# Moving the split weights of 256-column and 512-column products to different byte offsets in SBUF

## The chip, the cores and the metric

The kernel runs on one core of a Trainium2 chip. The metric is the device time of one execution in microseconds (us). Engines are called as in the profile: PE is TensorE (the matmuls; PEld is its loading of stationary weights), DVE is VectorE, ACT is ScalarE, POOL is GpSimd, SP is SyncE, which here only issues DMAs. SBUF is the on-chip memory of 128 partitions; an offset below is a number of bytes within one partition.

## The reference

One layer of a decoder trunk on x of 512 tokens by 1024, all in float32. Cut to what matters:

```python
h = rms_norm(x, g_mix)
qa, ka, va, qb, kb, vb, gates = split(h @ w_in)
ya = moba_attention(rope(qa), rope(ka), va)        # 8 heads of 64
yb = stick_breaking_attention(qb, kb, vb)          # 8 heads of 64
g = sigmoid(gates + b_gate)
x = x + (g[0] * (ya @ w_branch_a) + g[1] * (yb @ w_branch_b)) @ w_out
u = causal_depthwise_conv(rms_norm(x, g_ffn) @ w_up, conv_w, conv_b)
x = x + (silu(u_gate) * u_val) @ w_down            # w_up: 1024 x 5632, w_down: 2816 x 1024
return rms_norm(x, g_final)
```

Nearly all the work is in the products with w_in, w_branch, w_out, w_up and w_down.

## The kernel before

**Products.** Every float32 operand of a large product is split into two float32r tiles, `hi` (ACT copies the raw tile, line 74, 661 or 981) and `lo` = raw - hi (DVE, line 75, 661 or 983). `mm3` (lines 78 to 81) then makes three matmuls of each product: hi with hi, hi with lo, lo with hi. Each matmul has its own stationary operand of 128 by 128 (a block of 512 bytes in each partition), loaded while the matmul before streams its moving operand of 256 or 512 columns (1024 or 2048 bytes in each partition). The order of the matmuls on PE is the order of the program.

**Weights.** A DMA from SP brings a raw weight tile of 128 by 1024 into one of five `raw` buffers. The split weights `whi` and `wlo`, 4096 bytes each, come from the pool `wsp` (line 61), three buffers of each name in rotation. In some stages a split goes to other pools (`osp`, `dsp`) instead. The users of `wsp` are

- `wload` (line 62), for the first projections, the value projections, the queries, keys and gates, the branch products and the plain columns of w_up;
- `split_in` (line 658), for w_out and w_down;
- `upload` (line 803), for the first four tiles of w_up;
- `wmix` (line 972), for the mixed columns of w_up. For the last of its four tiles, `wd` (line 1004), hi and lo share one `whi` buffer.

**Which products have 256 columns.** Three places:

- `vproj_b` (line 301), the values of the second attention: the weights are the moving operand, the activations `xg` the stationary one. 2 groups x 4 token tiles x 8 blocks x 3 = 192 matmuls, spread as fillers between the steps of the attention.
- `up_half` (line 854), the first four tiles of w_up: the weights are stationary, half of `h2` moves. 4 tiles x 2 halves x 8 blocks x 3 = 192 matmuls; one of the four tiles lies in `osp`, the other three in `wsp`, so 144 of them read `wsp`.
- `first_four` and `last_three` (lines 986 and 1001), the mixed stage, 16 columns of tiles (`MIXED`, 4 to 19) that are computed with seven quarter products in place of eight: the weights are stationary, and quarters of `h2` or sums of them in `tm4` (called xa in the profile) move. 16 x 7 quarters x 4 blocks x 3 = 1344 matmuls, one after the other.

That makes 1728 matmuls of 256 columns, 1680 of them with weights from `wsp`. The other large products move 512 columns: 1461 matmuls with weights from `wsp` (weights stationary in `proj`, `up_mm` and the branch products, moving in the first value projection and in the products with w_out and w_down), and some 490 with weights from `osp` and `dsp` or none.

**Addresses.** In the program as laid out, all six buffers of `wsp`, and also `xg`, `h2`, `tm4`, `osp`, `dsp` and the split activations, begin at 320 bytes modulo 512. So every weight block and every activation block that meet in a product have the same offset modulo 512.

**What orders the work around.** SP loads raw tiles ahead, up to five; ACT copies as soon as a `whi` buffer comes free, which is when PE has done the last matmul on it; DVE subtracts after ACT; PE takes the tiles in program order. During the mixed stage, POOL issues loads and stores of its own. Of the mixed tiles, `wc` gets its `lo` by DMA from DRAM (`wlo<-ulo`), where an earlier stage has put it.

Of the kernel before, what the change touches and what calls it, by code (L numbers as in the profile page):

```python
# [10 lines left out]
F32 = mybir.dt.float32  # L11
F32R = mybir.dt.float32r
# [15 lines left out]
NP = FT // 2  # L28
# [11 lines left out]
          + [("di", j, i) for j in DSUM for i in range(3)])  # L40
WIDX = {k: i for i, k in enumerate(WORDER)}
NEG = -1e30


@with_exitstack
def trunk_layer(ctx: ExitStack, tc: tile.TileContext, x: bass.AP, xT: bass.AP, w: bass.AP, vec: bass.AP,
# [3 lines left out]
    def pool(stack, name, bufs, space=None, side=None):  # L50
        kw = {}
        if space is not None:
            kw["space"] = space
        if side is not None:
            kw["side"] = side
        return stack.enter_context(tc.tile_pool(name=name, bufs=bufs, reuse_waits="tile", **kw))
# [1 line left out]
    ctx.enter_context(tc.manual_schedule(engines={mybir.EngineType.PE}))  # L58
    consts = pool(ctx, "consts", 1)
    wraw = pool(ctx, "wraw", 5)  # L60
    wsp = pool(ctx, "wsp", 3)
    def wload(key, pieces=1, eng=None):
        raw = wraw.tile([128, 1024], F32, name="raw")
        hi = wsp.tile([128, 1024], F32R, name="whi")
        lo = wsp.tile([128, 1024], F32R, name="wlo")
        n = 1024 // pieces
        for i in range(pieces):
            sl = slice(i * n, (i + 1) * n)
            (eng if eng is not None and i == 0 else nc.sync).dma_start(raw[:, sl], w[WIDX[key]][:, sl])
            if eng is not None and i == 0:  # L70
                nc.scalar.preload_act_table_set("sqrt_and_others")
        for i in range(pieces):
            sl = slice(i * n, (i + 1) * n)
            wload.hi = nc.scalar.activation(hi[:, sl], raw[:, sl], AF.Copy)  # L74
            wload.lo = nc.vector.tensor_sub(lo[:, sl], raw[:, sl], hi[:, sl].bitcast(F32))  # L75
        return hi, lo

    def mm3(ps, a, b, start, stop, **kw):
        nc.tensor.matmul(ps, a[0], b[0], start=start, stop=False, **kw)  # L79
        nc.tensor.matmul(ps, a[0], b[1], start=False, stop=False, **kw)  # L80
        nc.tensor.matmul(ps, a[1], b[0], start=False, stop=stop, **kw)  # L81

    def blk(t, k, n=128):
        return t[0][:, k * n:(k + 1) * n], t[1][:, k * n:(k + 1) * n]
# [27 lines left out]
    vb = vp.tile([128, QT, 512], F32, name="vb")  # L112
# [34 lines left out]
    for n in NWARM:  # L147
        nc.tensor.matmul(warm[:, :n], warmb[:, :128], warmb[:, :n], start=True, stop=True)  # L148
    mf = xp.tile([128, 128], F32, name="mf", bufs=1)
    nc.gpsimd.memset(mf, 0.0)  # L150
    nc.gpsimd.affine_select(out=mf, in_=mf, pattern=[[-1, 128]], compare_op=OP.is_ge, fill=NEG, base=0,
                            channel_multiplier=1)
# [146 lines left out]
        yield 1.0  # L299

    def vproj_b(g):
        wt = tuple(wload(("vb", g, h)) for h in range(2))
        for t in range(QT):
            if t % 2 == 0:
                ps = pmm.tile([128, S], F32, name="mm")
            o = ps[:, (t % 2) * 256:(t % 2 + 1) * 256]
            for k in range(KT):
                a = (xg[k][:, 0, t * 128:(t + 1) * 128], xg[k][:, 1, t * 128:(t + 1) * 128])
                mm3(o, a, blk(wt[k // 4], k % 4, 256), k == 0, k == KT - 1)
                if k < KT - 1:  # L310
                    yield 0.5
            if t % 2:
                dst = vb[:, t - 1:t + 1, g * 256:(g + 1) * 256]
                nc.scalar.activation(dst[:, 0], ps[:, :256], AF.Copy, scale=r1[:, t - 1:t])
                nc.vector.tensor_scalar(dst[:, 1], o, r1[:, t:t + 1], None, op0=OP.mult)
            yield 0.5
# [216 lines left out]

    pend = {}
    fillers = [moba_qk(1), sb_qk(0), sb_qk(1), vproj_b(0), sb_qk(2), sb_qk(3), vproj_b(1)]
    fillers += [gates(i) for i in range(NG)]
    GAPS_A = (12, 0, 5, 5, 0, 5, 7, 5, 5)
# [61 lines left out]
    for i in range(KT):  # L599
# [5 lines left out]
        g = pend[i]  # L605
# [27 lines left out]
    t2 = [ocb.tile([128, 512], F32, name=f"ot{j}") for j in range(HP)]  # L633
# [6 lines left out]
    def rload(key):  # L640
        raw = wraw.tile([128, 1024], F32, name="raw")
        nc.sync.dma_start(raw, w[WIDX[key]])
        return raw
# [12 lines left out]
            next(todo, None)  # L656

    def split_in(p, raw):
        lo = p.tile([128, 1024], F32R, name="wlo")
        hi = p.tile([128, 1024], F32R, name="whi")  # L660
        splits.append((nc.scalar.activation(hi, raw, AF.Copy), nc.vector.tensor_sub(lo, raw, hi.bitcast(F32))))  # L661
        return hi, lo

# [5 lines left out]
    def first_pass(cq, j, n, xa, keys, t2, pools, last):  # L669
        if t2 is None:  # L670
            r1, r2 = (wraw.tile([128, 1024], F32, name="raw") for _ in range(2))
            nc.sync.dma_start(r2.rearrange("p (h c) -> p h c", h=2), keys[0][0:2].rearrange("h p c -> p h c"))
            nc.sync.dma_start(r1[:, :512], w[WIDX[keys[1]]][:, :512])
            nc.sync.dma_start(r1[:, 512:], keys[0][2])
        else:
            r0 = rload(keys[0])
            r1 = rload(keys[1])
            r2 = wraw.tile([128, 1024], F32, name="raw")
            nc.vector.tensor_add(r2, r0, r1)  # L679
            nc.vector.tensor_add(r1[:, 512:], r1[:, :512], r2[:, 512:])  # L680
            nc.scalar.activation(t2, r1[:, 512:], AF.Copy)
        w2 = split_in(pools[0], r2)
        w1 = split_in(pools[1], r1)
        for wt in (w2, w1):
            step(dsums if cq is oq else homes, wt[1][:, :1].bitcast(F32))
        steps = [("c22", 1, w2, 0), ("c21", 3, w2, 1), ("c11", 0, w1, 0), ("c12", 2, w1, 1)]
        if j == n - 1 and last:
            steps = steps[2:] + steps[1::-1]
        for m, b, wt, h in steps:
            prod(cq[m], xa, b, wt, h, j == 0, j == n - 1)  # L690
        return splits[-1]
# [109 lines left out]
    wup = []  # L801

    def upload(p):
        raw = rload(("up",) + upq.pop(0))
        wup.append((p.tile([128, 1024], F32R, name="whi"), p.tile([128, 1024], F32R, name="wlo"), raw))

    def upload_half(n, h):
        sl = slice(h * 512, (h + 1) * 512)
# [2 lines left out]
    def upload_hi(p):  # L811
        upload(p)
        nc.scalar.activation(wup[-1][0], wup[-1][2], AF.Copy)
# [5 lines left out]
    for j in range(HP):  # L819
# [7 lines left out]
        for n in ("c11", "c21") if j < HP - 1 else ("c21", "c11"):  # L827
# [3 lines left out]
    inline(*(lambda t=t: nc.vector.tensor_add(oq["c22"][t], oq["c22"][t], oq["u3", t]) for t in range(2)),  # L831
           *(lambda t=t: x1_add(t, 1) for t in (2, 3)), lambda: upload_hi(wsp))
    upload(wsp)
    inline(lambda: nc.scalar.activation(sqj[:, :1], padt[:, :1], AF.Sqrt), *(lambda t=t: x1_sq(t, 1) for t in (2, 3)))
    inline(*(lambda t=t, f=f: f(t, 0) for t in (2, 3) for f in (x1_add, x1_sq)), lambda: upload_lo(0))
# [44 lines left out]
    t2 = [gp.tile([128, 512], F32, name=f"t2{j}") for j in range(2)]  # L880
# [90 lines left out]

    def wmix(i, parts, n=1024, lo=None):
        raw = wraw.tile([128, 1024], F32, name="raw")
        hi = wsp.tile([128, 1024], F32R, name="whi")
        wlo = wsp.tile([128, 1024], F32R, name="wlo") if n == 1024 else hi[:, n:]
        for sl, src in parts:
            nc.sync.dma_start(raw[:, sl] if isinstance(sl, slice) else raw.rearrange("p (h c) -> p h c", h=2), src)
        if lo is not None:
            for h in (1, 0):
                nc.sync.dma_start(wlo[:, h * 512:(h + 1) * 512].bitcast(F32), lo[:, h].bitcast(F32))  # L980
        nc.scalar.activation(hi[:, :n], raw[:, :n], AF.Copy)  # L981
        if lo is None:
            nc.vector.tensor_sub(wlo, raw[:, :n], hi[:, :n].bitcast(F32))
        return hi, wlo
# [56 lines left out]
    cq = {n: [pd.tile([128, 512], F32, name=f"{n}{t}") for t in range(2)] for n in ("c11", "c21", "c12", "c22")}  # L1041
    acc = {(t, h): cq[f"c{t // 2 + 1}{h + 1}"][t % 2] for t in range(QT) for h in range(2)}
    t2p = pool(ctx, "t2p", 1, side="right")
    t2 += [t2p.tile([128, 512], F32, name=f"t2{j}") for j in range(2, NP)]
    dsp = [pool(ctx, "dsp0", 2, side="right")]
    nsplit = [0]

    def place():
        n = nsplit[0]
        nsplit[0] += 1  # L1050
        c = "wwwaaww"[n] if n < 7 else "bbwaaww"[n % 7]
        return wsp if c == "w" else dsp[c == "b"]
# [3 lines left out]
    for n, j in enumerate(order):  # L1056
        if n == 3:
            for split in splits2:
                if split:
                    split()  # L1060
            ust.close()
            dsp.append(pool(ctx, "dsp1", 2, side="right"))
        m = j in DSUM
        first_pass(cq, n, NP, xa[j], (dsum[j] if m else ("dx", j), ("down", 2 * j)), None if m else t2[n],
                   (place(), place()), True)
        if m:
            nc.gpsimd.dma_start(t2[n], dsum[j][3])
# [193 lines left out]
```

## Time and profile before

| what | value |
|---|---|
| median of 3 runs | 711.78 us (711.47 to 712.11) |
| the profiled execution's own time | 712.63 us |
| its span, first to last instruction | 710.9 us |
| outside the span | 1.7 us |
| PE busy | 702.3 us (99%) |
| PEld busy | 615.4 us (87%) |
| DVE busy | 575.2 us (81%) |
| ACT busy | 403.6 us (57%) |
| POOL busy | 130.6 us (18%) |
| mean granted TensorE clock | 0.997 |

Busy times are sums of the durations of an engine's instructions. PE's matmuls overlap each other in the record (one of 256 columns has a duration of 283 ns), so how fast PE goes is read from the distance between the starts of consecutive matmuls and not from durations. The chain in the profile follows the execution back from its last instruction to what released each step.

### The profile page before, as it was taken

How to read it: one execution, taken by the hardware profiler on the slowest of the kernel's cores; microseconds unless marked ns; L12 is line 12 of the kernel's file. 1: busy time of each engine (PE TensorE's matmuls, PEld its weight loads, DVE VectorE, ACT ScalarE, POOL GpSimd, SP SyncE). 2: the span in 40 equal slices, each digit the busy share in tenths (PEclk: the TensorE clock that was granted, in tenths of full speed). 3: DMA queues.
4: the chain of work that ended last, by engine and by line, in shares of the span. 5: the costliest groups of instructions: out<-in, count | busy, mean ns of one | idle time of the engine just before them, and what ended most of it. 6: DMA issues, size and time to landing. Idle time of an engine off the chain costs nothing.

```text
span 710.9 us, 11733 instructions
## 1 busy us (share of the span) xinstructions
PE 702.3 (99%) x4460; PEld 615.4 (87%) x4460; DVE 575.2 (81%) x901; ACT 403.6 (57%) x607; POOL 130.6 (18%) x200
## 2 busy tenths in 40 slices
PE   9999999999999999999999999999999999999995
PEld 6888888979888888888889899999999998888884
DVE  6778868597793868578795898989999998879987
ACT  6345445454563544456485657676676665456854
POOL 1211122233542222115514300000000002300000
PEclk9999999999999999999999999999999999999998
DMA  9699999999999788889998968888667665967703
GB/s 309 257 343 342 353 343 247 243 238 246 229 263 289 251 283 261 264 276 332 323 345 263 203 189 287 289 296 295 230 223 239 238 219 183 304 213 268 263 0 119
DMA packets 57577, 184.13 MB, mean 259 GB/s; under 512 B 6640, under 2 KB 7408, under 8 KB 51632
## 3 DMA queue, kind: packets, MB, share of 16 engines
q1 hardware_dynamic: 41136, 105.18, 42.7%
q0 software_dynamic: 16096, 77.87, 39.3%
q8 instruction: 35, 0.57, 0.3%
q10 hardware_dynamic: 288, 0.33, 0.1%
q14 instruction: 22, 0.18, 0.1%
HBM read 162.64 MB, written 64.75 MB: 320 GB/s over the span
## 4 chain that ended last, share of the span: by engine, by line
PE 98%; DVE 1%; ACT 0%; issue 0%; ACTq 0%
PE b L81 12%; PE b L80 12%; PE b L79 12%; PE mm L79 11%; PE mm L81 11%; PE mm L80 11%; PE c L79 5%; PE c L80 5%; PE c L81 5%; PE q L198 3%; PE tp L469 3%; PE tp L493 3%; PE sc L393 1%; PE sc L403 1%; PE mm L148 1%; PE v L79 1%
## 5 line engine op out<-in xcount | busy, mean ns | idle before, releaser
L79 PE MATMUL b<-h,whi 128*128 128x256 f32 (+1 forms) x320 | 97.4, 304 | 0.0
L80 PE MATMUL b<-h,whi 128*128 128x256 f32 (+1 forms) x320 | 97.4, 304 | 0.0
L81 PE MATMUL b<-h,wlo 128*128 128x256 f32 (+1 forms) x320 | 97.3, 304 | 0.0
L79 PE MATMUL mm<-xg,whi 128*128 128x512 f32 x224 | 89.8, 401 | 0.0
L74 ACT ACTIVATE whi<-raw 128x1024 fp32r<-128x1024 f32 (+2 forms) x62 | 59.7, 974 | 49.4 <-PE mm L81 16.9
L81 PE MATMUL mm<-xg,wlo 128*128 128x512 f32 x224 | 87.4, 390 | 0.0
L80 PE MATMUL mm<-xg,whi 128*128 128x512 f32 x224 | 87.3, 390 | 0.0
L981 ACT ACTIVATE whi<-raw 128x1024 fp32r<-128x1024 f32 x64 | 60.9, 951 | 46.1 <-PE b L80 31.1
L75 DVE TENSOR_TENSOR wlo<-raw,whi 128x1024 fp32r<-128x1024 f32 (+2 forms) x62 | 68.7, 1116 | 13.3 <-ACT whi L74 12.9
L79 PE MATMUL b<-xa,whi 128*128 128x256 f32 x256 | 72.4, 283 | 0.0
L80 PE MATMUL b<-xa,whi 128*128 128x256 f32 x256 | 72.4, 283 | 0.0
L661 ACT ACTIVATE whi<-raw 128x1024 fp32r<-128x1024 f32 x45 | 46.6, 1051 | 30.8 <-DVE raw L679 14.1
L80 PEld LDWEIGHTS b<-h,whi 128*128 128x128 f32 x320 | 61.2, 191 | 2.5
L79 PEld LDWEIGHTS b<-h,whi 128*128 128x128 f32 x320 | 61.2, 191 | 2.5
L81 PEld LDWEIGHTS b<-h,wlo 128*128 128x128 f32 x320 | 61.1, 191 | 2.5
L661 DVE TENSOR_TENSOR wlo<-raw,whi 128x1024 fp32r<-128x1024 f32 x45 | 54.7, 1221 | 5.4 <-ACT whi L661 5.0
L81 PE MATMUL b<-xa,wlo 128*128 128x256 f32 x192 | 54.3, 283 | 0.0
L79 PEld LDWEIGHTS mm<-xg,whi 128*128 128x128 f32 x224 | 42.1, 188 | 9.9 <-issue 1.8
L81 PEld LDWEIGHTS mm<-xg,wlo 128*128 128x128 f32 x224 | 42.0, 188 | 9.1
L655 POOL COPY small<-small 128x1 f32<-128x1 f32 x23 | 21.8, 975 | 151.6 <-DVE small L654 151.5
L79 PEld LDWEIGHTS b<-xa,whi 128*128 128x128 f32 x256 | 49.2, 192 | 0.0
L80 PEld LDWEIGHTS b<-xa,whi 128*128 128x128 f32 x256 | 49.2, 192 | 0.0
(282 smaller groups left out, 1780.1 us busy)
## 6 DMA issues: line engine op xcount, KB each, us to landing
raw<-w SPq DMA_DIRECT2D x103, 512.0 KB, 5.5
usum<-w POOLq DMA_DIRECT2D x16, 1024.0 KB, 25.9
raw<-usum SPq DMA_DIRECT2D x32, 512.0 KB, 4.6
usum<-w POOLq DMA_DIRECT2D x16, 512.0 KB, 19.8
usum<-usum POOLq DMA_DIRECT2D x32, 256.0 KB, 12.0
praw<-usum POOLq DMA_DIRECT2D x16, 512.0 KB, 5.8
ulo<-praw POOLq DMA_DIRECT2D x16, 512.0 KB, 5.5
wlo<-ulo SPq DMA_DIRECT2D x32, 256.0 KB, 4.1
```

The source lines that it names most:

```text
L74: wload.hi = nc.scalar.activation(hi[:, sl], raw[:, sl], AF.Copy)
L75: wload.lo = nc.vector.tensor_sub(lo[:, sl], raw[:, sl], hi[:, sl].bitcast(F32))
L79: nc.tensor.matmul(ps, a[0], b[0], start=start, stop=False, **kw)
L80: nc.tensor.matmul(ps, a[0], b[1], start=False, stop=False, **kw)
L81: nc.tensor.matmul(ps, a[1], b[0], start=False, stop=stop, **kw)
L148: nc.tensor.matmul(warm[:, :n], warmb[:, :128], warmb[:, :n], start=True, stop=True)
L198: nc.tensor.matmul(qk0[c], w0[i][:, (k % 2) * 512 + c * 128:(k % 2) * 512 + (c + 1) * 128], xg[k][:, j], start=(k == 0 and n == 0), stop=( ...
L469: nc.tensor.transpose(tp[:, h, c:c + 128], a[:, h, c:c + 128], ident)
L493: nc.tensor.matmul(av[h * 64:(h + 1) * 64, j, qt * 128:(qt + 1) * 128], v[:, kb, (2 * p + h) * 64:(2 * p + h + 1) * 64], aT[p][:, h, o + k ...
L655: with tc.issue_after(nc.gpsimd.tensor_copy(seen, seen).ins):
L661: splits.append((nc.scalar.activation(hi, raw, AF.Copy), nc.vector.tensor_sub(lo, raw, hi.bitcast(F32))))
L981: nc.scalar.activation(hi[:, :n], raw[:, :n], AF.Copy)
```

## The change

`wsp` is no longer one pool with three buffers of each of two names, but six pools with one buffer each. Each buffer is a little longer than the 1024 floats of a tile, 1040 or 1072, and a tile is a window of 1024 floats in it that begins at one of two places: `kind` 0 for products of 512 columns, `kind` 1 for products of 256. `kind` 1 is given in `vproj_b`, `upload` and `wmix`; everything else that uses `wsp` is `kind` 0. A tile `rest` of 64 floats, never written, fills the six pools up to a multiple of 512 bytes. Together they take 1024 bytes more than before, and to make room one buffer of 2048 bytes, the eleventh `t2` of the last stage, gets its place later, after the pool `up` has been closed.

The core of the diff:

```diff
+PLACES = ((1072, 0, 48), (1040, 16, 0), (1040, 0, 16), (1072, 48, 0), (1072, 0, 48), (1040, 16, 0))
...
-    wsp = pool(ctx, "wsp", 3)
-    def wload(key, pieces=1, eng=None):
+    wsp = [(pool(ctx, f"wsp{n}", 1), *at) for n, at in enumerate(PLACES)]
+    pool(ctx, "rest", 1).tile([128, 64], F32, name="rest")
+    nw = [0, 0]
+
+    def wtile(p, lo, kind=0):
+        if p is not wsp:
+            return p.tile([128, 1024], F32R, name="wlo" if lo else "whi")
+        q, size, *at = wsp[nw[lo] % 3 + 3 * lo]
+        nw[lo] += 1
+        return q.tile([128, size], F32R, name="wlo" if lo else "whi")[:, at[kind]:at[kind] + 1024]
+
+    def wload(key, pieces=1, eng=None, kind=0):
         raw = wraw.tile([128, 1024], F32, name="raw")
-        hi = wsp.tile([128, 1024], F32R, name="whi")
-        lo = wsp.tile([128, 1024], F32R, name="wlo")
+        hi = wtile(wsp, 0, kind)
+        lo = wtile(wsp, 1, kind)
...
     def vproj_b(g):
-        wt = tuple(wload(("vb", g, h)) for h in range(2))
+        wt = tuple(wload(("vb", g, h), kind=1) for h in range(2))
...
     def split_in(p, raw):
-        lo = p.tile([128, 1024], F32R, name="wlo")
-        hi = p.tile([128, 1024], F32R, name="whi")
+        lo = wtile(p, 1)
+        hi = wtile(p, 0)
...
     def upload(p):
         raw = rload(("up",) + upq.pop(0))
-        wup.append((p.tile([128, 1024], F32R, name="whi"), p.tile([128, 1024], F32R, name="wlo"), raw))
+        wup.append((wtile(p, 0, 1), wtile(p, 1, 1), raw))
...
     def wmix(i, parts, n=1024, lo=None):
         raw = wraw.tile([128, 1024], F32, name="raw")
-        hi = wsp.tile([128, 1024], F32R, name="whi")
-        wlo = wsp.tile([128, 1024], F32R, name="wlo") if n == 1024 else hi[:, n:]
+        hi = wtile(wsp, 0, 1)
+        wlo = wtile(wsp, 1, 1) if n == 1024 else hi[:, n:]
...
-    t2 += [t2p.tile([128, 512], F32, name=f"t2{j}") for j in range(2, NP)]
+    t2 += [t2p.tile([128, 512], F32, name=f"t2{j}") for j in range(2, NP - 1)]
...
             dsp.append(pool(ctx, "dsp1", 2, side="right"))
+            t2.append(pool(ctx, "t2q", 1, side="right").tile([128, 512], F32, name="t210"))
```

Adding up the lengths (modulo 512 bytes, against the first buffer's beginning, which is also the offset of all the activations) gives where a tile lies relative to the activations that it meets:

| buffer | begins at | kind 0 (512 columns) | kind 1 (256 columns) |
|---|---|---|---|
| hi, first | 0 | 0 | 192 |
| hi, second | 192 | 256 | 192 |
| hi, third | 256 | 256 | 320 |
| lo, first | 320 | 0 | 320 |
| lo, second | 0 | 0 | 192 |
| lo, third | 192 | 256 | 192 |

192 and 320 are 192 bytes to either side of 0 modulo 512. Before, all these were 0.

## The prediction

> **What bounds the kernel now.** I read the first part of the page, then the chain that ended last, then the timeline of PE.
>
> ```profile
> span 710.9 us, 11733 instructions
> PE 702.3 (99%) x4460; PEld 615.4 (87%) x4460; DVE 575.2 (81%) x901; ACT 403.6 (57%) x607; POOL 130.6 (18%) x200
> PE 98%; DVE 1%; ACT 0%; issue 0%; ACTq 0%
> ```
>
> PE is never without work, and the chain runs through it for 98% of the span: the kernel is as long as its 4460 matmuls follow each other. So what counts is the distance between the starts of consecutive matmuls. The timeline gives it in the mixed stage, where 1344 matmuls of 256 columns follow each other, 415.44 to 576.59; the row after them is the first of 512 columns.
>
> ```profile
> 415.21 0.39 PE L81 MATMUL b<-h,wlo 128*128 128x512 f32 x1
> 415.44 0.28 PE L79 MATMUL b<-h,whi 128*128 128x256 f32 x1
> 415.55 0.28 PE L80 MATMUL b<-h,whi 128*128 128x256 f32 x1
> ...
> 576.59 0.28 PE L81 MATMUL b<-xa,whi 128*128 128x256 f32 x1
> 576.71 0.40 PE L79 MATMUL b<-h,whi 128*128 128x512 f32 x1
> ```
>
> (576.71 - 415.44) / 1344 = 120.0 ns for each product of 256 columns. For 512 columns, seven consecutive starts (six distances, the first and the last shown):
>
> ```profile
> 364.16 0.39 PE L81 MATMUL b<-whi,xs 128*128 128x512 f32 x1
> ...
> 365.52 0.39 PE L81 MATMUL b<-whi,xs 128*128 128x512 f32 x1
> ```
>
> 1.36 / 6 = 226.7 ns. 256 more columns cost 106.7 ns, so 256 columns alone are 106.7, and each product pays a fixed 120.0 - 106.7 = 13.3 ns on top, at either width. That fixed part is all that the position of the weights could take away or add to. It is not the same everywhere. Right behind the transposes, where PE falls out of its rhythm, nine consecutive starts at 256 columns and seven at 512 (first and last shown, so eight and six distances):
>
> ```profile
> 120.26 0.28 PE L80 MATMUL mm<-wlo,xg 128*128 128x256 f32 x1
> ...
> 121.20 0.28 PE L79 MATMUL mm<-whi,xg 128*128 128x256 f32 x1
> 64.35 0.39 PE L80 MATMUL mm<-xg,whi 128*128 128x512 f32 x1
> ...
> 65.74 0.39 PE L80 MATMUL mm<-xg,whi 128*128 128x512 f32 x1
> ```
>
> 0.94 / 8 = 117.5 ns at 256 columns and 1.39 / 6 = 231.7 ns at 512, with the same shapes and the same addresses modulo 512. A few products later both widths are back in the rhythm above and stay in it. So the settled rhythm is the slower one for 256 columns and the faster one for 512. The distance depends on how the stream of the moving operand and the loading of the next weights stand to each other in time. The weight loads show it too:
>
> ```profile
> L79 PEld LDWEIGHTS b<-xa,whi 128*128 128x128 f32 x256 | 49.2, 192 | 0.0
> L79 PEld LDWEIGHTS mm<-xg,whi 128*128 128x128 f32 x224 | 42.1, 188 | 9.9 <-issue 1.8
> ```
>
> The same 128 by 128 load takes 192 ns beside 256 columns and 188 beside 512. Both streams read SBUF, one at about twice the speed of the other, and both start at the same offset modulo 512. That a shift of one against the other changes the fixed part is therefore plausible; no row of this trace has another offset for such a product.
>
> **The change part by part.** It adds and removes no instruction on any engine and no DMA. Three things move.
>
> *The 256-column products.* 1680 of them read weights at 192 or 320 bytes from the other operand, where it was 0: 1344 in the mixed stage, 192 in the second value projection, 144 in the first tiles of w_up. The bounds of one product are 0 and 13.3 ns saved (no stall below the streaming of the columns is possible), or 0 to 22.4 us in all; a loss can't be excluded, and the nearest row for it is the 5.0 ns that a product of 512 columns pays out of rhythm (231.7 - 226.7). Between the ends I take the middle, 6.67 ns, a distance of 113.3. The rows that it is nearest to are the 117.5 ns above and the very first distance of the mixed stage, 415.55 - 415.44 = 110 ns at this view's step of 10; both lie below 120. A second reason: 120.0 and 226.7 are 18 and 34 times 6.67, so the two rhythms look like whole steps, and the next lower step is 17, or 113.3. That is 1344 x 6.67 = 8.96, 192 x 6.67 = 1.28 and 144 x 6.67 = 0.96, together 11.2 us.
>
> What becomes late then is DVE. The mixed stage in the windows (PE, PEld, DVE, ACT and POOL busy after the length):
>
> ```profile
> 415.00:576.00 161.00, 161.00 (x1342) 160.92 (x1341) 146.11 (x227) 112.10 (x168) 4.37 (x8) 1.00 0.76 257
> DVE whi L983 <- ACT whi L981: 7.9, 11, 1.7
> DVE t L901 <- ACT t L900: 3.4, 10, 0.9
> DVE wlo L983 <- ACT whi L981: 2.5, 4, 1.6
> ACT whi L981 <- PE b L80: 30.2, 29, 2.0
> ACT whi L981 <- PE b L81: 6.6, 13, 0.5
> ```
>
> DVE works 146.1 of 161.0 us there. At 113.3 ns PE would want the stage done in 152.3, which leaves DVE 6.2 us of idle time where its waits for ACT now sum to 13.8 (7.9 + 3.4 + 2.5, from the list of waits of that stretch). If none of these shrank, PE would have to wait 13.8 - 6.2 = 7.6 us; but most of them end with an ACT copy that itself waits for PE to free a buffer (36.8 us of such waiting), and come earlier when PE is earlier. I take a quarter, 2.0 us given back, with 0 and 7.6 as ends. Net gain 9.2 us.
>
> *The 512-column products from wsp.* Where they lie at 0 as before nothing changes. Following the rotation of the buffers through the program, 792 of the 1461 lie at 256 bytes from the other operand. Bounds: 5.0 ns lost each (the 231.7 above), 4.0 us; or one step of 6.67 ns gained, 5.3 us. I take 0, because blocks of weights are 512 bytes long and half a block off brings the two streams, one twice as fast as the other, to the same place once per product as before.
>
> *Layout.* All that lies behind `wsp` moves by 1024 bytes, which leaves its offset modulo 512 alone; `t210` is taken later. It is first written by the last of the eight copies of this row:
>
> ```profile
> L681 ACT ACTIVATE t<-raw x8: 611/632/635, 607.3 to 646.5; 128x512 f32<-128x512 f32 x8
> ```
>
> 646.5 lies far behind the end of the mixed columns, whose buffers it takes, so I cost it at nothing. If the later place did make that copy wait, the subtraction and products of one weight tile would be queued behind it, and it would cost about one copy and one subtraction:
>
> ```profile
> L661 ACT ACTIVATE whi<-raw 128x1024 fp32r<-128x1024 f32 x45 | 46.6, 1051 | 30.8 <-DVE raw L679 14.1
> L661 DVE TENSOR_TENSOR wlo<-raw,whi 128x1024 fp32r<-128x1024 f32 x45 | 54.7, 1221 | 5.4 <-ACT whi L661 5.0
> wlo<-ulo SPq DMA_DIRECT2D x32, 256.0 KB, 4.1
> ```
>
> That is 1.05 + 1.22 = 2.3 us, the bound above; the one below is 0, since no wait goes away. The copies, subtractions and the 32 loads of `wlo` write the same bytes to other offsets. I take them at their present lengths; the loads are issued a tile ahead, and their 4.1 us lie beside about 3 us of products on the tile before and the raw tile's own load.
>
> Sum: the profiled execution would take 712.63 - 9.2 = 703.4 us; the median lies 0.85 below it, so I expect 702.6.
>
> **A rule beside these rows.** The distances above are 120.0 and 226.7 ns. The Trainium skill (TensorE: Matmul & The Clock Gate, section "Back-to-back issue gap") gives an isolated gap of columns / 2.4 + 2.5 ns, or 109.2 and 215.8. By that page 10.8 ns of each product would be stall, and removing all of it would give 1680 x 10.8 = 18.2 us, an estimate from that page. The trace's 256-column slope (106.7) agrees with 2.4 columns per ns; no run here shows the 2.5.
>
> **The rivals.**
>
> *All the fixed part goes.* Then the mixed stage would be PE-bound at 1344 x 106.7 = 143.4 us, less than DVE's 146.1, so DVE becomes the bound and the gain there stops at 161.3 - 146.1 = 15.2 us; the other 336 products give 4.5. With the same 2.0 given back: 17.7, or 694.1 us. Against it: DVE would need a stage without a gap.
>
> *Only the lock is broken.* Two offsets, mixed between hi and lo, may keep PE out of rhythm: 117.5 ns, 2.5 x 1680 = 4.2 us, 707.6.
>
> *Nothing changes.* The 13.3 ns are equal for both widths and for every tile, which a fixed cost of exchanging the weights would explain; then 711.8. Against it are the 117.5 and 231.7 ns of the same shapes. The Trainium skill (SBUF — State Buffer, section "Who interferes with whom") gives PE two independent read ports, one for the moving operand and one for the weights, and says that PE never waits on anyone; by that rule offsets would change nothing, 711.8. The varying distances of this trace speak against it, though no row here shows their cause.
>
> *Slower: the 512-column products lose their rhythm.* 226.7 is the fast state for them, and 792 get another offset. At 231.7 they cost 4.0 us: 715.8 if the 256-column products gain nothing. It decides from the point where those gain less than 4.0 / 1680 = 2.4 ns each, which is just what breaking the lock would give.
>
> **How the numbers follow.** About 0.2%, 1.4 us, is what a measurement of this kernel can tell from no change. The forecast (one step, 700.5 to 705.5) has 0.40; all of it, 0.12; the lock only, 0.18; nothing, 0.14; slower, 0.16. So faster 0.70, same 0.14, slower 0.16. The range runs from 694, the full gain with DVE as bound, to 713, the end of no change, and leaves out the slower case and a sliver below.
>
> **What would show it.** In the profile after, the 1344 starts of the mixed stage at 113 ns apart; six distances of 512 columns still 1.36 us, with weights at 0 and at 256; the weight loads beside 256 columns back at 188 ns; DVE above 95% busy in the mixed stage, with some PE waits on `wlo` or `whi`. Distances of 120.0 there would make the forecast wrong, distances of about 117 would show the lock alone, and 231 in the 512-column stages the slower rival.

## The result and the profile after

The changed kernel takes 701.96 us (median of 4 runs, 701.36 to 702.77) against 711.94 for the kernel before in the same comparison (4 runs, 711.47 to 712.56). The ratio is 0.986, with a 95% interval of 0.9843 to 0.9877: faster by 10.0 us, where 9.2 was forecast (702.6).

The page of the changed kernel. Its lines are the old ones plus 11.

```profile
span 699.6 us, 11729 instructions
PE 690.9 (99%) x4460; PEld 604.3 (86%) x4460; DVE 573.7 (82%) x901; ACT 404.3 (58%) x607; POOL 123.8 (18%) x200
PE 98%; DVE 1%; ACT 1%; DMA 1%; issue 0%; ACTq 0%
```

PE is still the chain from end to end. The timeline of PE shows two products of 512 columns, six distances apart; then the mixed stage, its first product and the first of 512 columns behind it (start and duration in us stand first):

```profile
362.46 0.39 PE L92 MATMUL b<-whi,xs 128*128 128x512 f32 x1
...
363.82 0.39 PE L92 MATMUL b<-whi,xs 128*128 128x512 f32 x1
...
412.98 0.28 PE L90 MATMUL b<-h,whi 128*128 128x256 f32 x1
...
565.31 0.40 PE L90 MATMUL b<-h,whi 128*128 128x512 f32 x1
```

The six distances of 512 columns take 1.36 us as before. In the mixed stage (565.31 - 412.98) / 1344 = 113.3 ns, where it was 120.0. The weight loads beside 256 columns are back at the length that they have beside 512:

```profile
L90 PEld LDWEIGHTS b<-xa,whi 128*128 128x128 f32 x256 | 48.1, 188 | 0.0
```

What DVE does in the mixed stage now, in the windows (PE, PEld, DVE, ACT, POOL busy behind the length), and the waits of that stretch:

```profile
413.00:565.00 152.00, 152.00 (x1343) 152.00 (x1342) 144.61 (x226) 111.97 (x168) 4.39 (x8) 1.00 0.79 272
DVE t L912 <- ACT t L911: 3.2, 10, 0.9
DVE whi L994 <- ACT whi L992: 2.1, 6, 1.2
DVE wlo L994 <- ACT whi L992: 1.3, 2, 1.1
```

DVE is 95% busy (144.61 of 152), and its waits for ACT have shrunk from 13.8 us to 6.6. PE is busy all of the 152 us, and the list of waits of that stretch has no row of PE or PEld, so nothing is given back.

To split the gain by stage, these rows of the chain are landmarks: the 80 matmuls with which the first and the fourth attention step end. Before (the first fence) and after (the second):

```profile
91.90 4.52 PE tp L493 x80
222.44 4.52 PE tp L493 x80
```

```profile
90.82 4.52 PE tp L504 x80
220.75 4.52 PE tp L504 x80
```

| stretch | before, us | after, us | gain | what of 256 columns is in it |
|---|---|---|---|---|
| start to the first landmark | 91.90 | 90.82 | 1.08 | nothing |
| first to fourth landmark | 130.54 | 129.93 | 0.61 | second value projection, 192 |
| to the mixed stage (415.44, 412.98) | 193.00 | 192.23 | 0.77 | first tiles of w_up, 144 |
| mixed stage (to 576.71, 565.31) | 161.27 | 152.33 | 8.94 | 1344 |
| the rest (to 710.9, 699.6) | 134.2 | 134.3 | -0.1 | nothing |

The 1.08 us at the start are not counted to the change. In the timeline of PE these are the first eight large products before, after, and in `u0`, the first experiment below, which has the offsets of before:

```profile
4.98 3.13 PE L198 MATMUL q<-xg,whi 128*128 128x512 f32 x8
```

```profile
4.85 2.12 PE L209 MATMUL q<-xg,whi 128*128 128x512 f32 x8
```

```profile
4.98 2.55 PE L209 MATMUL q<-xg,whi 128*128 128x512 f32 x8
```

The same eight products take 3.13, 2.12 and 2.55 us. Before and `u0` have the same offsets and differ by 0.58 us here, so the offsets alone do not set it. What does, these profiles don't show: the granted clock reads 1.00 from 4 to 7 us in all three. The profiled execution of before, 712.63 us, is also longer than any of its timed ones, and that of after, 701.36 us, is the shortest of its four. Without the start the profiles differ by 11.3 - 1.1 = 10.2 us, and the medians by 10.0.

### The profile page after: what moved, and what is told of

Read it like the earlier page. It is cut to its first block, busy times and chain, and to the rows that moved or that the text cites. A ratio compares the mean times of both kernels' runs of the same rounds, so it can differ in the third digit from the quotient of the medians.

```text
span 699.6 us, 11729 instructions
## 1 busy us (share of the span) xinstructions
PE 690.9 (99%) x4460; PEld 604.3 (86%) x4460; DVE 573.7 (82%) x901; ACT 404.3 (58%) x607; POOL 123.8 (18%) x200
## 4 chain that ended last, share of the span: by engine, by line
PE 98%; DVE 1%; ACT 1%; DMA 1%; issue 0%; ACTq 0%
PE b L92 12%; PE b L90 12%; PE b L91 12%; PE mm L90 11%; PE mm L92 11%; PE mm L91 11%; PE c L91 5%; PE c L90 5%; PE c L92 5%; PE q L209 3%; PE tp L480 3%; PE tp L504 3%; PE sc L404 1%; PE sc L414 1%; PE v L91 1%; PE v L90 1%
## 5 line engine op out<-in xcount | busy, mean ns | idle before, releaser
L90 PE MATMUL b<-h,whi 128*128 128x256 f32 (+1 forms) x320 | 95.8, 299 | 0.0
L91 PE MATMUL b<-h,whi 128*128 128x256 f32 (+1 forms) x320 | 95.7, 299 | 0.0
L92 PE MATMUL b<-h,wlo 128*128 128x256 f32 (+1 forms) x320 | 95.7, 299 | 0.0
L90 PE MATMUL b<-xa,whi 128*128 128x256 f32 x256 | 70.7, 276 | 0.0
L91 PE MATMUL b<-xa,whi 128*128 128x256 f32 x256 | 70.7, 276 | 0.0
L90 PEld LDWEIGHTS b<-h,whi 128*128 128x128 f32 x320 | 60.1, 188 | 2.5
L91 PEld LDWEIGHTS b<-h,whi 128*128 128x128 f32 x320 | 60.1, 188 | 2.5
L90 PEld LDWEIGHTS mm<-xg,whi 128*128 128x128 f32 x224 | 42.1, 188 | 9.9 <-issue 1.8
L91 PEld LDWEIGHTS mm<-xg,whi 128*128 128x128 f32 x224 | 42.2, 188 | 7.9
L91 PEld LDWEIGHTS b<-xa,whi 128*128 128x128 f32 x256 | 48.1, 188 | 0.0
L90 PEld LDWEIGHTS b<-xa,whi 128*128 128x128 f32 x256 | 48.1, 188 | 0.0
```

## The experiments

In all of them the name "place" means the offset of the weights in `wsp` relative to the activations, modulo 512. Each kernel is the changed one with another `PLACES` line and another length of `rest`, so that each keeps the six pools and the late `t210`; what else an edit changes is shown with it, and where it adds or takes out a line, line numbers differ by one. Two rows of the timeline are shown for each: the first product of the mixed stage and the first behind it, 1344 products apart. The distance at 512 columns is taken between the same two products of the branch and w_out stages in every kernel, 500 apart. It is an average over three kinds: in 370 of the 500 the weights are stationary and at the place, in 54 they are the moving operand, so that the stationary block lies the place's bytes to the other side, and in 76 they come from other pools and stay at 0.

**Layout alone.** All tiles at 0:

```diff
-PLACES = ((1072, 0, 48), (1040, 16, 0), (1040, 0, 16), (1072, 48, 0), (1072, 0, 48), (1040, 16, 0))
+PLACES = ((1024, 0, 0),) * 6          # and 128 floats in "rest"
```

> Six pools as in the changed kernel, the late place of t210 and 512 bytes of padding, but every tile at offset 0 relative to the activations: the layout of the change without its offsets. If the offsets are the cause, the mixed stage goes at 120.0 ns a product again, 512 columns at 226.7, and the time is that of before, about 711.9 us. If layout (the pools, the late t210) brought the gain, about 702.

```profile
414.82 0.28 PE L90 MATMUL b<-h,whi 128*128 128x256 f32 x1
...
576.09 0.40 PE L90 MATMUL b<-h,whi 128*128 128x512 f32 x1
```

161.27 / 1344 = 120.0 ns, and 712.16 us beside 712.27 for the kernel before. The pools and the late buffer bring nothing; the gain comes from the offsets.

**One place for everything, 64, 128 and 192 bytes.** The first buffer is lengthened by 16, 32 or 48 floats and its window begins there, which moves all six (`rest` is as much shorter than the 128 floats of the kernel above):

```diff
+PLACES = ((1040, 16, 16),) + ((1024, 0, 0),) * 5     # 64 bytes; 32 and 48 floats for 128 and 192
```

> All tiles of wsp, of both widths, at 64 bytes relative to the activations. Theory (the place where the two streams meet decides): one place for each width; 64 bytes are 6.67 ns of the moving operand and 13.3 ns of the weights, so 256 columns stay near the old meeting place, 117 to 120 ns, and 512 columns leave their best place, up to 231.7. First rival (any offset but 0 will do): 113.3 in the mixed stage. Second rival (it takes two offsets, mixed between hi and lo): 120.0.

```profile
246.64 0.39 PE L92 MATMUL mm<-yb,wlo 128*128 128x512 f32 x1
...
362.73 0.39 PE L91 MATMUL b<-w,xs 128*128 128x512 f32 x1
...
419.58 0.28 PE L90 MATMUL b<-h,whi 128*128 128x256 f32 x1
...
571.90 0.39 PE L90 MATMUL b<-h,whi 128*128 128x512 f32 x1
```

> All tiles of wsp at 128 bytes. Theory: 256 columns between 113.3 and 120 ns, 512 columns above 226.7. First rival (any offset): 113.3 and no change at 512. Second rival (the mixture of two offsets): 120.0.

```profile
420.83 0.28 PE L90 MATMUL b<-h,whi 128*128 128x256 f32 x1
...
580.32 0.39 PE L90 MATMUL b<-h,whi 128*128 128x512 f32 x1
```

> All tiles of wsp at 192 bytes, one offset for hi and lo and for both widths. Theory: the mixed stage at 113.3 ns as after the change, and 512 columns slower than 226.7, which is what the second place of each tile is for: at 231.7 the 1461 products would lose 7.3 us, so about 709 in all. First rival (any offset): 113.3 at 256 and 226.7 at 512, 702. Second rival (the mixture): 120.0 at 256 columns, 712 or more.

```profile
244.78 0.39 PE L92 MATMUL mm<-yb,wlo 128*128 128x512 f32 x1
...
359.36 0.39 PE L91 MATMUL b<-w,xs 128*128 128x512 f32 x1
...
416.23 0.28 PE L90 MATMUL b<-h,whi 128*128 128x256 f32 x1
...
574.53 0.39 PE L90 MATMUL b<-h,whi 128*128 128x512 f32 x1
```

At 64: 152.32 / 1344 = 113.3 ns, and 116.09 / 500 = 232.2 ns at 512 columns; 709.41 us. At 128: 159.49 / 1344 = 118.7 and 231.7; 717.78. At 192: 158.30 / 1344 = 117.8 and 114.58 / 500 = 229.1; 711.86. So the place matters at both widths, and "any offset will do" is out. But two expectations of my own theory missed: 64 was to stay near 120 and gave 113.3, and 192, which the change itself uses, gave 117.8 when it is the only one.

**The other half of the circle, 256, 320, 384 and 448 bytes.** The same edit with 64, 80, 96 and 112 floats.

> All tiles of wsp at 256 bytes, half a block off. The changed kernel has 792 of its 512-column products there and they went at 226.7 ns, so 512 columns: 226.7, unless that came from their lying between tiles at 0. 256 columns: by the theory that the meeting place of the two streams decides, half a block off meets once as at 0, 120.0; by the rival that any offset helps, 113 to 118.

```profile
415.36 0.28 PE L90 MATMUL b<-h,whi 128*128 128x256 f32 x1
...
576.63 0.40 PE L90 MATMUL b<-h,whi 128*128 128x512 f32 x1
```

> All tiles of wsp at 320 bytes, the other of the two places that the change uses for 256 columns. At 192 alone the mixed stage went at 117.8 ns and not at 113.3 as in the changed kernel, where 192 and 320 are mixed. If 320 alone is the fast one, 113.3 here; if it takes the mixture, 117 to 118 again. 512 columns: about 229 as at 192.

```profile
420.54 0.28 PE L90 MATMUL b<-h,whi 128*128 128x256 f32 x1
...
572.86 0.39 PE L90 MATMUL b<-h,whi 128*128 128x512 f32 x1
```

> All tiles of wsp at 384 bytes, that is 128 to the other side of 0. If the distance depends on the size of the offset alone, as at 128: 118.7 at 256 columns, 232.5 at 512, about 718 us. If the sign matters (the weights ahead of the moving operand or behind it), another value.

```profile
420.95 0.28 PE L90 MATMUL b<-h,whi 128*128 128x256 f32 x1
...
580.44 0.39 PE L90 MATMUL b<-h,whi 128*128 128x512 f32 x1
```

> All tiles of wsp at 448 bytes, that is 64 to the other side of 0. If the size of the offset alone decides, as at 64: 113.4 at 256 columns with stationary weights, 233 at 512, about 709 us. If the sign matters, another value.

```profile
417.17 0.28 PE L90 MATMUL b<-h,whi 128*128 128x256 f32 x1
...
575.46 0.39 PE L90 MATMUL b<-h,whi 128*128 128x512 f32 x1
```

| place, bytes | 256 columns, mixed stage, ns | 512 columns, ns | time, us (one run) |
|---|---|---|---|
| 0 and 256 | 120.0, 120.0 | 226.7, 226.7 | 712.16, 712.64 |
| 64 and 320 | 113.3, 113.3 | 232.2, 232.2 | 709.41, 710.36 |
| 128 and 384 | 118.7, 118.7 | 231.7, 231.7 | 717.78, 718.21 |
| 192 and 448 | 117.8, 117.8 | 229.1, 229.1 | 711.86, 712.79 |

In all four pairs the pattern repeats after 256 bytes, not 512; 512 columns losing nothing at 256 is one of them. In this scan it has no mirror: 64 and 448, equally far from 0, differ by 4.4 ns, so the expectation from the size of the offset alone missed at 448 and held at 384, which is 128 in any reading. The expectation at 320 missed too: 512 columns took 232.2 ns and not the 229 of 192. Put into the period of 256, the change mixes the places 192 (117.8 in this scan) and 64.

The column of 512 columns holds the three kinds named above. With stationary weights alone, in the 96 products right ahead of the mixed stage, it is 233.4 ns at 64 and 320, 232.4 at 128 and 384, 228.9 at 192 and 448.

**Half a step.** All tiles are at 32 bytes (8 floats).

> All tiles of wsp at 32 bytes, half the smallest shift so far. If the distance changes in whole steps at every 64 bytes (256 columns 120.0 at 0, 113.3 at 64): one of these two. If it runs evenly between them: about 116.7. If a better place lies between: below 113.3, down to 106.7 if a whole step goes. 512 columns with stationary weights between 226.7 and 233.4.

```profile
420.72 0.28 PE L90 MATMUL b<-h,whi 128*128 128x256 f32 x1
...
579.77 0.40 PE L90 MATMUL b<-h,whi 128*128 128x512 f32 x1
```

159.05 / 1344 = 118.3 ns, 232.5 at 512 columns, 718.07 us. Neither of the two steps, and not the even 116.7; it is not a better place.

**Difference or place.** Weights and activations moved together by 192 bytes, so that all blocks begin at 0 modulo 512: 48 floats ahead of the raw buffers, and 80 more in the pad on the other side of SBUF.

```diff
+    pool(ctx, "front", 1).tile([128, 48], F32, name="front")
     wraw = pool(ctx, "wraw", 5)
-    padt = pad.tile([128, 40], F32, name="padt")
+    padt = pad.tile([128, 120], F32, name="padt")
```

> Weights and activations all moved together by 192 bytes: the difference stays 0 everywhere, but every block now begins at 0 modulo 512. If the difference between the two operands decides: 120.0 and 226.7 ns, about 712 us. If the place of each alone decides (a block that does not cross a multiple of 512 or 256 bytes): 113 ns in the mixed stage and another value at 512 columns, 702 or less.

```profile
414.56 0.28 PE L91 MATMUL b<-h,whi 128*128 128x256 f32 x1
...
575.84 0.40 PE L91 MATMUL b<-h,whi 128*128 128x512 f32 x1
```

161.28 / 1344 = 120.0 ns, 226.7 at 512 columns, 711.92 us. At this common shift, the only one tried and with a difference of 0, the place of each operand by itself changes nothing.

**256 columns at 192 alone, 512 columns at 0.** This takes the same memory as the change, and one line of edit. Of the six buffers two, the third of hi and the first of lo, have their window at 448, which is 192 again in the period of 256.

```diff
+PLACES = ((1072, 0, 48), (1040, 16, 0)) * 3
```

> The changed kernel with 512-column weights at 0 or 256 and all 256-column weights at 192 or 448 (the same place if the pattern repeats every 256 bytes), so without the mixture with 320. Theory (each place has its own rhythm, and the tiles at 320 hold PE in the rhythm of 113.3): the mixed stage at 117.8 ns, 4.4 ns x 1488 = 6.5 us above the changed kernel, about 708.5 us. Rival (the 512-column products around it, now back at 0, bring PE into the good rhythm): 113.3, about 702.

```profile
413.40 0.28 PE L90 MATMUL b<-h,whi 128*128 128x256 f32 x1
...
571.69 0.40 PE L90 MATMUL b<-h,whi 128*128 128x512 f32 x1
```

158.29 / 1344 = 117.8 ns, and 707.62 us (one run). This is what the theory that each place has its rhythm expected; the 512-column products at 226.7 around the stage do not bring it to 113.3.

**Each kind at its best place.** Stationary 256-column weights at 64 or 320, the moving ones of the value projection at 192 or 448, 512 columns at 0 or 256. The tile `rest` is left out, so the memory is the same:

```diff
+PLACES = ((1072, 0, 16, 48), (1056, 16, 32, 0), (1072, 48, 0, 32)) * 2
-        wt = tuple(wload(("vb", g, h), kind=1) for h in range(2))
+        wt = tuple(wload(("vb", g, h), kind=2) for h in range(2))
```

> A third place for each tile, in the same memory: 512 columns at 0 or 256, stationary 256-column weights all at 64 or 320, moving ones (second value projection) at 192 or 448, each the best of the scan. By the scan: mixed stage 113.3 as in the changed kernel, value projection 116.0 against about 116.3 there, first tiles of w_up 113.4. So about 0.1 us below the changed kernel, 702, ratio to before 0.986. If the mixture of 192 and 320 was worth more than 320 alone, above it.

```profile
413.79 0.28 PE L89 MATMUL b<-h,whi 128*128 128x256 f32 x1
...
572.08 0.40 PE L89 MATMUL b<-h,whi 128*128 128x512 f32 x1
```

158.29 / 1344 = 117.8 ns, not 113.3. 707.63 us (median of 4 runs, 707.12 to 708.10) against 712.25 (7 runs), ratio 0.9936 (0.9919 to 0.9952), where the changed kernel has 0.986. "Each place has its own rhythm" falls here. The weights lie as in the kernel at 64 alone, up to the 256 bytes that made no difference there, and go 4.4 ns slower.

What it is instead stands earlier in the same kernel, in `up_half`. Its last 120 products are 24 on the fourth tile of w_up, then 24 on each of the first, second, third and fourth. In this kernel all lie at 64 or 320 but the third, which is in `osp` at 0. Starts in the first three groups (60 distances), then in the last (18 distances):

```profile
379.04 0.28 PE L91 MATMUL b<-h,wlo 128*128 128x256 f32 x1
...
385.84 0.28 PE L91 MATMUL b<-h,wlo 128*128 128x256 f32 x1
...
389.41 0.28 PE L91 MATMUL b<-h,wlo 128*128 128x256 f32 x1
...
391.53 0.28 PE L91 MATMUL b<-h,wlo 128*128 128x256 f32 x1
```

6.80 / 60 = 113.3 ns and 2.12 / 18 = 117.8 ns. The fourth tile is in both: the very same weights at the same place take 113.3 ns a product the first time and 117.8 the second, with 24 products at 0 just ahead. So there are two rhythms at the place 64, and which of them PE holds goes with how it came in.

The kernel at 64 alone does the same on these tiles, and shows what differs at the mixed stage. Its last group of `up_half` (18 distances), and the first of the 96 products of 512 columns that lie between `up_half` and the mixed stage:

```profile
394.58 0.28 PE L92 MATMUL b<-h,wlo 128*128 128x256 f32 x1
...
396.70 0.28 PE L92 MATMUL b<-h,wlo 128*128 128x256 f32 x1
...
397.17 0.40 PE L90 MATMUL b<-h,whi 128*128 128x512 f32 x1
```

2.12 / 18 = 117.8 ns, and, with its mixed stage beginning at 419.58, (419.58 - 397.17) / 96 = 233.4. Both kernels leave `up_half` in the slower rhythm. The 96 products that follow lie at 64 there and at 0 or 256 here, where they go at about 227 ns, and behind them the mixed stage runs at 113.3 there and at 117.8 here.

The changed kernel has two rhythms at 192. There the fourth tile has hi and lo at 192, and opens and closes the same 120 products (18 distances in each):

```profile
377.55 0.28 PE L92 MATMUL b<-h,wlo 128*128 128x256 f32 x1
...
379.67 0.28 PE L92 MATMUL b<-h,wlo 128*128 128x256 f32 x1
...
388.70 0.28 PE L92 MATMUL b<-h,wlo 128*128 128x256 f32 x1
...
390.74 0.28 PE L92 MATMUL b<-h,wlo 128*128 128x256 f32 x1
```

2.12 / 18 = 117.8 and 2.04 / 18 = 113.3. Between them come the first tile, with hi at 320 and lo at 192, the second, with hi at 192 and lo at 320, and the third at 0. The rhythm goes over to 113.3 within the first three products on the first tile and is back at 113.3 right behind the third. The mixed stage begins with a tile of hi at 192 and lo at 320, is at 113.3 from the fourth product on and keeps it through all 1344, tiles with hi and lo at 192 included. Without a tile whose hi and lo differ in this way, the three kernels that had 192 alone (192, 448, and the two together) ran the whole mixed stage in the slow rhythm.

But the place 192 can have the faster rhythm without that mixture. In the kernel with 192 and 448 the first 48 products of `up_half`, on two tiles with one of hi and lo at 192 and the other at 448, come right behind products of 512 columns. Their first, and the first product behind them:

```profile
367.37 0.28 PE L90 MATMUL b<-h,whi 128*128 128x256 f32 x1
...
372.81 0.28 PE L90 MATMUL b<-h,whi 128*128 128x256 f32 x1
```

5.44 / 48 = 113.3 ns. Behind the third tile, at 0, the same kernel then runs the fourth at 117.8, stays at that when it comes to the same two tiles again, and runs the mixed stage at it. It also shows that more than the last few products ahead can count: in both kernels the last group on the fourth tile follows 24 products at 0, and it goes at 113.3 in the changed kernel and at 117.8 in this one. Since 64 and 192 each hold both rhythms, the 4.4 ns between them in the scan at 256 columns are a difference of rhythm and no fixed property of the two places.

That two rhythms exist at one place, and that the entry goes with which one PE holds, is shown by these rows. That a tile with 192 and 320 mixed takes PE out of the slower one is what the going over at the first such tile points to, where the kernel without 320 stays; whether a single such tile at the start of the stage would be enough wasn't tried.

## Why the prediction came out right, point by point

- *PE's distances bound the kernel.* Right: the chain is PE for 98% in both kernels, and the gain is in the distances.
- *One step of 6.67 ns of the 13.3.* Right in the stage that carries it: 120.0 to 113.3 over 1344 products, 8.94 us against 8.96. The grounds were weaker than the hit. The middle of two ends was chosen with the argument of whole steps. The argument holds for this rhythm, but the same places also hold 117.8, and the prediction had nothing to tell which of the two the stage would run in: of the mixture of 192 and 320 it said only that it might keep PE out of rhythm. That it came out at 113.3 was in this respect luck. With 192 for all of it, the rival "only the lock is broken" would have come true almost to the figure: 117.8 ns and 707.6 us measured, 117.5 and 707.6 forecast.
- *The weight loads.* They came back to 188 ns as forecast, but that is no sign of 113.3: the kernel with all tiles at 128 has 188 too, at 118.7 ns a product, and the kernel with 192 and 448 has 187 and 188 at 117.8.
- *192 and 144 products beside it, 1.28 and 0.96 us.* Too much: 0.61 and 0.77. The value projection, with moving weights between transposes, hardly settles (0.61 us in 192 products, 3.2 ns for each), and the first 24 of the last 120 products of `up_half` ran at 117.8.
- *2.0 us given back through DVE.* Mis-sized: 0. DVE is 95% busy as forecast, but its waits for ACT shrank from 13.8 us to 6.6, and no PE wait appeared. This and the point above work against each other: without the 0.9 us too much, and with nothing given back, the sum is 11.2 - 0.9 = 10.3, against 10.2 in the profiles and 9.2 forecast.
- *512-column products, nothing.* Right: 226.7 at 0, at 256 and mixed. In the program as built 808 of 1488 of them lie at 256, where the prediction counted 792 of 1461, which at equal distances changes nothing. The reason given, that half a block off meets the same way, fits the period of 256 bytes; no run tests it further. The slower rival did not come in here, but its price is real: with stationary weights at 64 and at 128 these products take 6.7 and 5.7 ns more, and the kernels at 128 and 384 were 5.5 and 6.1 us slower than the kernel before in spite of faster 256-column products.
- *Layout, nothing.* Right: 712.16 beside 712.27 with the layout alone.
- *The rules of the Trainium skill.* By the isolated gap of the Trainium skill (TensorE: Matmul & The Clock Gate, section "Back-to-back issue gap"), 109.2 ns for 256 columns, 18.2 us were to be had, an estimate from that page; 10 came, and no settled distance goes below 113.3. By the rule of the Trainium skill (SBUF — State Buffer, section "Who interferes with whom") that PE's two read ports are independent and that PE never waits on anyone, nothing was to change. The measurement differs: with nothing changed but the difference between the offsets of the two operands, the same products take 113.3 to 120.0 ns, and 226.7 to 233.4 at 512 columns. What in SBUF or PE makes the distance depend on that difference, no run here shows.

## What to carry to other kernels

In a kernel whose PE goes without a gap, read the distance between starts of equal matmuls, not their durations: here the same shapes took 113.3 to 120.0 ns with the offset of the stationary block against the moving one modulo 256 bytes, and with what ran ahead of them. Try a few offsets in steps of 64 bytes, for each width by itself: in the scan here the place of the fastest stage at 256 columns (64) was about the slowest for 512, and the fastest for 512 (0) the slowest for 256. A place that is best in a scan may run in another rhythm when it is put together with others, as the version of best places did, so time the whole. And a place that is slow in a scan may have a faster rhythm, as 192 does, so a scan with one entry does not tell what a place can do.

## What the runs showed of the hardware that was not expected

In the mixed stage the averages of all settled rhythms are whole numbers of steps of 6.67 ns over a few products: 17 and 18 for one product at 113.3 and 120.0, 53 for three at 117.8, 89 for five at 118.7, 142 for eight at 118.3. In the starts of the trace the pattern of distances repeats after five products at 128 bytes and after eight at 32. At 512 columns 226.7 is 34 such steps and the 233.3 that settles at 64 (the last 72 of the 96 products ahead of the mixed stage) is 35. What the step is, no run here shows.

A rhythm, once taken, can hold for over a thousand products across changes of tile and place (1344 at 113.3 through places 192 and 320). So the same weights at the same place, modulo 256 bytes, took 113.3 ns or 117.8 with what ran ahead of the stage, which over 1344 products is 6.0 us.
